# The first stretch of a two-layer f32 network on one core: three projection tiles in step, group 0's scan spread over two groups, lo halves on GpSimd

## The chip, the core and the metric

The kernel runs on one NeuronCore of a Trainium2 chip. The core has TensorE (PE: matrix products, operands from SBUF, results into PSUM), VectorE (DVE) and ScalarE (ACT) for elementwise work, GpSimd (POOL), and SyncE (SP), from whose queue nearly all transfers from device memory are issued. Each engine works through its own queue in order and waits on semaphores for the others. The metric is the device time of one execution in microseconds (us).

## The reference

Input x is 512 positions of 1024 features, f32. Two layers add to it, each on `rms_norm(h)`; a last norm follows. The first layer, the scan layer, is what the change touches:

```python
proj = u @ in_w                      # z, x, B, C and dt, side by side
xbc = silu(causal_depthwise_conv(xbc, conv_w, conv_b))
dt = softplus(dt_raw + dt_bias);  a = dt * -exp(a_log)
y = ssd_chunked(xs * dt[..., None], a, b_in, c_out)   # 4 chunks of 128, 32 heads, 8 groups
y = y + d_skip * xs
y = gated_group_rms_norm(y, z, norm_w, 8)
return y @ out_w
```

In a chunk, `ssd_chunked` multiplies the products of C and B by decays exp(cum(a)_t - cum(a)_s) and applies them to x; between chunks a state of 128 x 64 per head is carried on. The second layer is a latent attention with 16 heads, which the change leaves alone.

## The kernel before

**Numbers in two halves.** A weight or activation of 32 bits is cut into a high half (`hi`, a rounded copy by ACT, line 272 for weights) and a low half (`lo`, the difference by DVE, line 273). A product is three matmuls, hi x hi, hi x lo and lo x hi (`passes`). A tile of the projection, 128 output columns by 512 positions, is 8 blocks of 128 features and so 24 matmuls of 512 columns.

**Groups.** The scan layer has 8 groups. Each needs six tiles: B, C, x0, x1, z0, z1. `ssm_in(g)` issues these as a generator, six matmuls a step; `sched` runs it and starts other pieces of work when the matmuls issued so far (at 0.216 us each) reach a number in a table: `S0P` for the projection of group 0, `P0` for the work beside group 1's projection, `P1` for the later groups. These pieces are group g's scan (beside the projection of group g + 1): `cb` (transposes of B, products of C and B, decays L times cb), `x(0)` and `x(1)` (transposes, then `xdt` and `xw` on DVE), `states` (matmuls on `xw`, line 105, and the carried states S), and `y` (matmuls, lines 130 and 138, then the gate on DVE). `GN` places the group norm. So the order on every engine is written out by hand through these numbers; within it a scheduler may shift instructions on the other engines' queues.

**The first group.** The input's norm is not known at first. B, C, x0 to z1 of group 0, and the first four tiles of group 1, are computed from `vh`, `vl`, the halves of x times the norm's weight, and multiplied by 1/rms (`rr`, lines 322 to 324) when they leave PSUM. 1/rms comes from squares (ACT) summed on DVE, a product with ones on PE (`pssq`), a logarithm and an exponential on ACT, and three steps on DVE. `ssm_dt` computes dt in five steps; its first product `d`, times `rr`, is transposed on PE (line 504) before all the rest.

**Buffers.** Weights land in `raw` (2 buffers, 512 KB each, loaded from SP's queue at line 263). There are three `hi`, three `lo` buffers, and three PSUM banks for tiles (`mm`), three `aux`, two `yd`. `weight(i)` splits one tile ahead and loads one more. A `raw` buffer is free when both its halves are made, a `hi` buffer when PE has done the tile's 24 matmuls.

**The start.** x arrives as eight tiles; before, B and C of group 0 are computed together, x tile by x tile (`gemm2`, line 300), from weights that arrive in quarters of 128 KB per two x tiles. Then x0 follows on its own.

Of the kernel before, what the change touches and what calls it, by code (L numbers as in the profile page):

```python
# [10 lines left out]
F32 = mybir.dt.float32  # L11
F32R = mybir.dt.float32r
# [38 lines left out]
OA = 8  # L51
SQ = 2


# [97 lines left out]
class Net:  # L152
# [99 lines left out]
    def prefetch(self, want):  # L252
        while self.wload < min(want + 1, len(self.wq)):
            self.wraws.append(self.load_weight(*self.wq[self.wload]))
            self.wload += 1
        while self.wpos < min(want, len(self.wq)):
            self.wready[self.wq[self.wpos]] = list(self.split_weight(self.wraws.pop(0)))[-1]
            self.wpos += 1
# [6 lines left out]

    def split_weight(self, raw, cuts=()):
        nc = self.nc
# [3 lines left out]
        for a, b in zip((0, *cuts), (*cuts, n)):  # L271
            nc.scalar.copy(hi[:, a:b], raw[:, a:b])  # L272
            nc.vector.tensor_tensor(lo[:, a:b], raw[:, a:b], hi[:, a:b].bitcast(F32), op=ALU.subtract)  # L273
            yield
        yield hi, lo
# [19 lines left out]
    def gemm2(self, ps, ws, xh, xl, ks):  # L295
        seqs = [self.passes(w, xh, xl, ks) for w in ws]
        for k in range(ks):
            for p, seq in zip(ps, seqs):
                for i in range(3 * k, 3 * k + 3):
                    self.nc.tensor.matmul(p, seq[i][0], seq[i][1], start=i == 0, stop=i == 3 * ks - 1)  # L300
            yield 6 * 0.216

# [34 lines left out]
    def sumsq(self, tiles, n, pstag, pool=None, tags=("r0", "rt", "rr"), after=None):  # L337
        nc = self.nc
        acc = None
        for x in tiles:  # L340
# [19 lines left out]
    def ssm(self):  # L360
# [12 lines left out]
        self.wload = 2  # L373
        for k in range(KD):
            x = self.res.tile([P, T], F32, tag="res", name=self.nm("x"))
            nc.sync.dma_start(x[:], t["x"][k])
            self.xs.append(x)
            if k % 2 == 0:
                s = slice(k * P, (k + 2) * P)
                for i, raw in enumerate(raws):  # L380
                    nc.sync.dma_start(raw[:, s], t["w"][i, :, s])
        wdt = wk.tile([P, KD, NH], F32, name="wdt", bufs=1)
# [9 lines left out]

        vh, vl = [], []
        ws = [self.split_weight(raw, (256, 512, 768)) for raw in raws]
        for k in range(KD):
            a = self.o16.tile([P, T], F32R, tag="o", name=self.nm("vh"))
            b = self.o16.tile([P, T], F32R, tag="o", name=self.nm("vl"))
            last = nc.scalar.activation(a[:], self.xs[k][:], AF.Copy, scale=nw[:, k:k + 1])
            if k % 2 == 0:
# [6 lines left out]
        for i, w in enumerate(ws):  # L406
            self.wready[self.wq[i]] = next(w)
        self.wpos = 2
# [24 lines left out]
        for g in range(NG):  # L433
            ys, q = [], []
            pieces = [] if g == 0 else [(GN, late)]
            if g == 0:
                begin = lambda: q.append(SSD(self, 0, self.lexp(0), ys))
                pieces += [(SU[0] + SU[1] * k, scaled) for k in range(KD)]
                pieces += [(P0[0], step), (P0[1], step), (P0[1] + 0.1, begin)]
                at = P0[2:]  # L440
            else:
                q.append(SSD(self, g, self.lexp(g), ys))
                at = P1
            pieces += [(at[0], lambda: q[0].cb()), (at[1], lambda: q[0].x(0)), (at[2], lambda: q[0].x(1)),
                       (at[3], lambda: q[0].states()), (at[4], lambda: q[0].y())]
            if g + 1 < NG:
# [118 lines left out]
    def ssm_in(self, g, uh, ul, early):  # L565
# [3 lines left out]
        for i, (name, ct) in enumerate((("B", 16 + g), ("C", 24 + g), ("x0", 2 * g), ("x1", 2 * g + 1),  # L569
                                        ("z0", 0), ("z1", 0))):  # L570
            pair = (0, 1) if g == 0 and i < 2 else (4, 5) if g == NG - 1 and i >= 4 else None
            w = None if pair and i == pair[1] else self.weight("w", U_IN + 6 * g + i)
            xh, xl, r = early[:3] if i < early[3] else (uh, ul, None)
# [4 lines left out]
            if pair:  # L578
                if i == pair[0]:
                    two = [ps, self.mm()]  # L580
                    ws = [w, self.weight("w", U_IN + 6 * g + i + 1)]
                    yield from self.gemm2([p[:] for p in two], ws, xh, xl, KD)
# [489 lines left out]
```

## Time and profile before

| | |
|---|---|
| median of 3 runs | 840.74 us (840.42 to 841.0) |
| the profiled execution | 840.15 us, span 838.3 |
| PE busy, share of span | 822.8 us, 98% |
| DVE busy | 640.2 us, 76% |
| ACT busy | 453.5 us, 54% |
| POOL busy | 0.2 us, 4 instructions |

The page gives busy time per engine, waits by pair of instructions, and groups of like instructions by source line; the timeline gives single instructions with their start, length, and, in brackets, how long the engine was idle before and who released it. PE's instructions are pipelined, so the distance of their starts tells more than their length. Tile names are shown without their buffer numbers. DMA rows of SP show the issue; the time to landing is in the list of DMA issues.

### The profile page before, as it was taken

How to read it: one execution, taken by the hardware profiler on the slowest of the kernel's cores; microseconds unless marked ns; L12 is line 12 of the kernel's file. 1: busy time of each engine (PE TensorE's matmuls, PEld its weight loads, DVE VectorE, ACT ScalarE, POOL GpSimd, SP SyncE). 2: the span in 40 equal slices, each digit the busy share in tenths (PEclk: the TensorE clock that was granted, in tenths of full speed). 3: DMA queues.
4: the chain of work that ended last, by engine and by line, in shares of the span. 5: the costliest groups of instructions: out<-in, count | busy, mean ns of one | idle time of the engine just before them, and what ended most of it. 6: DMA issues, size and time to landing. Idle time of an engine off the chain costs nothing.

```text
span 838.3 us, 11586 instructions
## 1 busy us (share of the span) xinstructions
PE 822.8 (98%) x4260; PEld 694.8 (83%) x4260; DVE 640.2 (76%) x1226; ACT 453.5 (54%) x802; POOL 0.2 (0%) x4
## 2 busy tenths in 40 slices
PE   7999999999999999999999999999999999999996
PEld 5887888888888888888888888888888888888885
DVE  7899898979788979776564887786767869675544
ACT  7567755545565657333354664456547557554233
POOL 0000000000000000000000000000000000000000
PEclk9999999999999999999999999999999999999999
DMA  6354543434242424323225242222221224331212
GB/s 227 102 186 145 153 150 106 147 101 128 98 151 76 151 87 137 121 95 101 90 86 176 79 129 64 77 65 73 73 64 56 89 75 157 100 100 53 92 59 100
DMA packets 35112, 90.55 MB, mean 108 GB/s; under 512 B 4784, under 2 KB 6320, under 8 KB 35056
## 3 DMA queue, kind: packets, MB, share of 16 engines
q1 hardware_dynamic: 34336, 88.77, 32.9%
q10 hardware_dynamic: 720, 1.05, 0.3%
q8 instruction: 33, 0.54, 0.3%
q14 instruction: 23, 0.19, 0.1%
HBM read 83.12 MB, written 4.33 MB: 104 GB/s over the span
## 4 chain that ended last, share of the span: by engine, by line
PE 91%; DVE 5%; DMA 2%; ACT 1%; issue 1%; SPq 0%; DVEq 0%; ACTq 0%
PE mm L291 54%; PE ot L942 11%; PE s L794 5%; PE mm L300 4%; PE po L836 4%; PE mm L774 3%; PE pt L818 2%; PE yd L138 2%; PE yd L291 1%; PE aux L130 1%; PE aux L105 1%; DMA x<-in_x_dram 1%; PE aux L77 1%; PE aux L89 1%; DMA L<-ac_d 1%; DVE wlo L273 1%
## 5 line engine op out<-in xcount | busy, mean ns | idle before, releaser
L272 ACT CAST whi<-raw 128x1024 fp32r<-128x1024 f32 (+3 forms) x132 | 127.0, 965 | 214.7 <-PE mm L291 177.4
L273 DVE TENSOR_TENSOR wlo<-raw,whi 128x1024 fp32r<-128x1024 f32 (+3 forms) x132 | 146.8, 1115 | 56.1 <-ACT whi L272 55.8
L291 PE MATMUL mm<-ah,whi 128*128 128x512 f32 x384 | 153.9, 401 | 0.0
L291 PE MATMUL mm<-ah,wlo 128*128 128x512 f32 x384 | 150.1, 391 | 0.4 <-DVE wlo L273 0.4
L291 PE MATMUL mm<-al,whi 128*128 128x512 f32 x384 | 149.8, 390 | 0.0
L291 PE MATMUL mm<-vh,whi 128*128 128x512 f32 x224 | 89.6, 400 | 0.9 <-ACT whi L272 0.9
L291 PE MATMUL mm<-vh,wlo 128*128 128x512 f32 x224 | 87.8, 392 | 0.7 <-DVE wlo L273 0.7
L291 PE MATMUL mm<-vl,whi 128*128 128x512 f32 x224 | 87.5, 391 | 0.0
L291 PEld LDWEIGHTS mm<-ah,wlo 128*128 128x128 f32 x384 | 72.1, 188 | 16.0 <-DVE wlo L273 0.8
L291 PEld LDWEIGHTS mm<-ah,whi 128*128 128x128 f32 x384 | 72.2, 188 | 15.5 <-issue 1.4
L291 PEld LDWEIGHTS mm<-al,whi 128*128 128x128 f32 x384 | 72.2, 188 | 14.4 <-DVE al L312 0.3
L942 PE MATMUL ot<-whi,ah 128*128 128x512 f32 (+1 forms) x136 | 52.3, 384 | 0.0
L942 PE MATMUL ot<-whi,al 128*128 128x512 f32 (+1 forms) x136 | 51.4, 378 | 0.0
L942 PE MATMUL ot<-wlo,ah 128*128 128x512 f32 (+1 forms) x136 | 51.4, 378 | 0.0
L291 PEld LDWEIGHTS mm<-vh,wlo 128*128 128x128 f32 x224 | 42.0, 188 | 10.8 <-DVE wlo L273 1.5
L291 PEld LDWEIGHTS mm<-vh,whi 128*128 128x128 f32 x224 | 42.1, 188 | 9.2 <-ACT whi L272 1.1
L223 ACT ACTIVATE p<-p,st 128x128 f32<-128x128 f32 (+1 forms) x64 | 36.1, 564 | 25.1 <-DVE st L806 25.0
L291 PEld LDWEIGHTS mm<-vl,whi 128*128 128x128 f32 x224 | 42.2, 188 | 7.2
L822 ACT CAST ph<-pt 128x512 fp32r<-128x512 f32 (+1 forms) x64 | 26.5, 422 | 33.2 <-PE pt L818 32.8
L291 PE MATMUL mm<-ch,whi 128*128 128x512 f32 x104 | 42.6, 409 | 0.0
L291 PE MATMUL mm<-ch,wlo 128*128 128x512 f32 x104 | 40.8, 392 | 0.0
L291 PE MATMUL mm<-cl,whi 128*128 128x512 f32 x104 | 40.7, 392 | 0.0
(225 smaller groups left out, 1642.6 us busy)
## 6 DMA issues: line engine op xcount, KB each, us to landing
raw<-in_w_dram SPq DMA_DIRECT2D x100, 512.0 KB, 3.3
L<-ac_d SPq DMA_DIRECT2D x32, 256.0 KB, 3.8
E<-ea_d SPq DMA_DIRECT2D x32, 128.0 KB, 3.3
raw<-in_ua_dram SPq DMA_DIRECT2D x8, 512.0 KB, 3.3
raw<-in_ub_dram SPq DMA_DIRECT2D x8, 320.0 KB, 2.9
x<-in_x_dram SPq DMA_DIRECT2D x8, 256.0 KB, 4.3
res<-in_x_dram SPq DMA_DIRECT2D x8, 256.0 KB, 3.3
hd<-ht SPq DMA_DIRECT2D x8, 256.0 KB, 2.3
```

The lines of the kernel that those rows point to most:

```text
L138: nc.tensor.matmul(yd[64 * h:64 * h + 64, s], self.xdt[j][:, c, h, :], self.L[2 * j + h][:, s], start=True, stop=True)
L223: i = self.nc.scalar.activation(out, in_, func, **k)
L272: nc.scalar.copy(hi[:, a:b], raw[:, a:b])
L273: nc.vector.tensor_tensor(lo[:, a:b], raw[:, a:b], hi[:, a:b].bitcast(F32), op=ALU.subtract)
L291: self.nc.tensor.matmul(ps, a, b, start=i == 0, stop=i == len(seq) - 1)
L300: self.nc.tensor.matmul(p, seq[i][0], seq[i][1], start=i == 0, stop=i == 3 * ks - 1)
L774: nc.tensor.matmul(ps[:, c2 * 256:(c2 + 1) * 256], a, b, start=i == 0, stop=i == 5)
L794: nc.tensor.matmul(ps[:, :n], x[:, s], y[:, :n], start=k == 0, stop=k == 4)
L818: nc.tensor.transpose(pt[:, (b - kb) * P:(b - kb + 1) * P], probs[h][b][:, kb * P:(kb + 1) * P], self.ident)
L822: nc.scalar.copy(ph[:, :n], pt[:, :n])
L836: nc.tensor.matmul(po[:, kb * P:], x, y, start=kb == 0 and k == 0, stop=kb == NCH - 1 and k == 2)
L942: nc.tensor.matmul(ps[:, a:b], x, y, start=start and i == 0, stop=stop and i == 5)
```

## The change

Four things change together.

1. In the first stretch B, C and x0 of group 0 go in step (`gemm2` on three tiles). The third weight's quarters land in two activation buffers that are not in use yet. The squares of x are interleaved with the splitting instead of following it.
2. Eight matmuls on a tile of zeros (128 x 128) stand at the head of PE's queue.
3. Group 0's scan is spread: `cb`, `x(0)`, `x(1)` stay in group 1's projection, but later; `states` and `y` move to group 2's, where group 1's whole scan also follows later than before (`PL`, `PM`, `GM`). dt's steps move too (`S0P`, `P0`).
4. The lo halves of the other 45 weight tiles of the scan layer's projection are subtracted by POOL instead of DVE (`prefetch`, `split_weight`).

```diff
-S0P = (13.82, 14.2, 15.4, 15.6, 17.62)
+S0P = (15.5, 15.51, 15.52, 15.53, 24.2)
 SU = (0.64, 1.42)
-P0 = (6.0, 6.8, 11.91, 15.25, 17.25, 24.88, 34.5)
+P0 = (12.5, 14.0, 19.4, 22.5, 24.0)
+PL = (2.0, 7.0)
+PM = (12.0, 13.4, 14.8, 21.0, 27.0)
+GM = 29.5
...
+            engine = self.nc.gpsimd if self.wpos < 6 * NG else self.nc.vector
+            self.wready[self.wq[self.wpos]] = self.split_weight(self.wraws.pop(0), engine)
...
+        self.nc.scalar.copy(hi[:], raw[:])
+        engine.tensor_tensor(lo[:], raw[:], hi[:].bitcast(F32), op=ALU.subtract)
+        return hi, lo
...
-                self.link(i, [after])
+                self.link(i, [after[k]])
...
+        idle = wk.tile([P, P], F32, name="idle", bufs=1)
+        nc.vector.memset(idle[:], 0.0)
+        pw = aux()
+        for _ in range(WARM):
+            nc.tensor.matmul(pw[:, :P], idle[:], idle[:], start=True, stop=True)
...
+        third = [self.act.tile([P, T], F32, tag=g, name=self.nm("raw")) for g in ("ah", "al")]
+        raws.append([third[k // 2][:, (k % 2) * 2 * P:(k % 2 + 1) * 2 * P] for k in range(KD // 2)])
...
-            pss = self.sumsq([x[:] for x in self.xs], D, "aux", after=last)
+            pss = self.sumsq([x[:] for x in self.xs], D, "aux", after=[marks[min(k + 3, KD - 1)] for k in range(KD)])
...
+            elif g == 1:
+                pieces += [(PL[0], lambda: first[0].states()), (PL[1], lambda: first[0].y()), (PL[1] + 0.1, begin)]
+                at = PM
...
-            pair = (0, 1) if g == 0 and i < 2 else (4, 5) if g == NG - 1 and i >= 4 else None
+            pair = (0, 1, 2) if g == 0 and i < 3 else (4, 5) if g == NG - 1 and i >= 4 else None
```

The instructions as they stand on the engines, at three places. First, ACT's queue around the logarithm that starts 1/rms (`r<-pssq`). The casts of weight tiles around it make their `hi` halves: before, `whi_188`, `whi_242`, `whi_396` are those of x0, x1 and z0 of group 0. Before:

```order
L272 CAST whi_188<-raw_182 128x1024
L342 ACTIVATE sq_293<-x_113 128x512
L272 CAST whi_242<-raw_186 128x1024
L342 ACTIVATE sq_296<-x_115 128x512
L342 ACTIVATE sq_299<-x_119 128x512
L353 CAST sqh_302<-sqa_277 128x512
L272 CAST whi_396<-raw_240 128x1024
L223 ACTIVATE r_54_309<-pssq_306 128x512
L223 ACTIVATE r_54_309<-r_54_309 128x512
L272 CAST whi_434<-raw_394 128x1024
```

And now, where `whi_216`, `whi_381`, `whi_455` are x1, z0, z1:

```order
L355 ACTIVATE sq_338<-x_136 128x512
L275 CAST whi_216<-raw_212 128x1024
L366 CAST sqh_341<-sqa_316 128x512
L275 CAST whi_381<-raw_214 128x1024
L275 CAST whi_455<-raw_379 128x1024
L227 ACTIVATE r_56_348<-pssq_345 128x512
L227 ACTIVATE r_56_348<-r_56_348 128x512
L275 CAST whi_488<-raw_453 128x1024
```

In both, three weight casts precede the logarithm; they are now those of the tiles x1, z0 and z1, and the squares end ahead of them.

Second, SP's queue at the loads of these tiles, with the semaphores that each waits for (DVE, Pool: the engine that made the halves from the buffer's last content; DMAHW: earlier transfers). Before:

```order
L263 DMA raw_182<-in_w_dram 128x1024 [waits DMAHW6_49,DVE_49]
L263 DMA raw_186<-in_w_dram 128x1024 [waits DMAHW7_49,DVE_49]
L263 DMA raw_240<-in_w_dram 128x1024 [waits DMAHW6_49,DMAHW0_49,DVE_49]
L263 DMA raw_394<-in_w_dram 128x1024 [waits DMAHW7_49,DMAHW1_49,DVE_49]
L263 DMA raw_432<-in_w_dram 128x1024 [waits DMAHW2_49,DMAHW0_49,DVE_49]
```

Now:

```order
L268 DMA raw_212<-in_w_dram 128x1024 [waits DMAHW2_49,DVE_49]
L268 DMA raw_214<-in_w_dram 128x1024 [waits DMAHW3_49,DVE_49]
L268 DMA raw_379<-in_w_dram 128x1024 [waits DMAHW4_49,DMAHW2_49,Pool_49]
L268 DMA raw_453<-in_w_dram 128x1024 [waits DMAHW5_49,DMAHW3_49,Pool_49]
L268 DMA raw_486<-in_w_dram 128x1024 [waits DMAHW6_49,DMAHW4_49,Pool_49]
```

From the third load on they wait for POOL instead of DVE.

Third, SP's queue at the loads of group 1's decays (`L<-ac_d`, broadcast from device memory). Before, they stand behind loads of weight tiles that wait for DVE and ACT; `PE` is the last reader of the four L buffers:

```order
L263 DMA raw_838<-in_w_dram 128x1024 [waits DMAHW3_49,DVE_49,Activation_49]
L263 DMA raw_949<-in_w_dram 128x1024 [waits DMAHW0_49,DMAHW4_49,DVE_49,Activation_49]
L263 DMA raw_1018<-in_w_dram 128x1024 [waits DMAHW5_49,DMAHW3_49,DVE_49]
L627 DMA L_919<-ac_d 128x512 [waits DMAHW6_49,PE_49]
L627 DMA L_927<-ac_d 128x512 [waits DMAHW7_49,PE_49]
```

Now:

```order
L268 DMA raw_885<-in_w_dram 128x1024 [waits DMAHW7_49,Pool_49]
L268 DMA raw_934<-in_w_dram 128x1024 [waits DMAHW1_49,DMAHW0_49,Pool_49]
L268 DMA raw_1042<-in_w_dram 128x1024 [waits DMAHW7_49,Pool_49]
L268 DMA raw_1111<-in_w_dram 128x1024 [waits DMAHW2_49,DMAHW0_49,Pool_49]
L653 DMA L_995<-ac_d 128x512 [waits DMAHW3_49,DVE_49,PE_49]
L653 DMA L_1003<-ac_d 128x512 [waits DMAHW4_49,DVE_49,PE_49]
```

They stand behind the loads of group 2's x0, x1, z0 and z1 (`raw_885` to `raw_1111`), each of which waits for POOL.

More of the change, by code (lines that the diff above doesn't have):

```diff
@@ L52 @@
 SQ = 2
+WARM = 8
 class SSD:
@@ L264, in load_weight, with split_weight @@
         return raw
[L266 to L267 removed]
+    def split_weight(self, raw, engine):
         n = raw.shape[1]
@@ L270, in split_weight, with split_first @@
         lo = self.wlo.tile([P, n], F32R, tag="lo", name=self.nm("wlo"))
-        for a, b in zip((0, *cuts), (*cuts, n)):
-            nc.scalar.copy(hi[:, a:b], raw[:, a:b])
-            nc.vector.tensor_tensor(lo[:, a:b], raw[:, a:b], hi[:, a:b].bitcast(F32), op=ALU.subtract)
+        self.nc.scalar.copy(hi[:], raw[:])
+        engine.tensor_tensor(lo[:], raw[:], hi[:].bitcast(F32), op=ALU.subtract)
+        return hi, lo
+    def split_first(self, raw):
+        nc = self.nc
+        hi = self.whi.tile([P, D], F32R, tag="hi", name=self.nm("whi"))
+        lo = self.wlo.tile([P, D], F32R, tag="lo", name=self.nm("wlo"))
+        for k, part in enumerate(raw):
+            s = slice(2 * k * P, 2 * (k + 1) * P)
+            nc.scalar.copy(hi[:, s], part)
+            nc.vector.tensor_tensor(lo[:, s], part, hi[:, s].bitcast(F32), op=ALU.subtract)
             yield
@@ L339, in sumsq @@
         acc = None
-        for x in tiles:
+        for k, x in enumerate(tiles):
             sq = self.nrm.tile([P, T], F32, tag="sq", name=self.nm("sq"), bufs=SQ)
@@ L570, in ssm_in @@
                                         ("z0", 0), ("z1", 0))):
-            pair = (0, 1) if g == 0 and i < 2 else (4, 5) if g == NG - 1 and i >= 4 else None
-            w = None if pair and i == pair[1] else self.weight("w", U_IN + 6 * g + i)
+            pair = (0, 1, 2) if g == 0 and i < 3 else (4, 5) if g == NG - 1 and i >= 4 else None
+            w = None if pair and i != pair[0] else self.weight("w", U_IN + 6 * g + i)
             xh, xl, r = early[:3] if i < early[3] else (uh, ul, None)
@@ L579, in ssm_in @@
                 if i == pair[0]:
-                    two = [ps, self.mm()]
-                    ws = [w, self.weight("w", U_IN + 6 * g + i + 1)]
+                    two = [ps] + [self.mm() for _ in pair[1:]]
+                    ws = [w] + [self.weight("w", U_IN + 6 * g + k) for k in pair[1:]]
                     yield from self.gemm2([p[:] for p in two], ws, xh, xl, KD)
```

28 lines of the change are left out of this document (15 added, 13 removed).

## The prediction

> **What bounds the kernel now.** I read the head of the page first, then TensorE's (PE's) waits, then busy time by stretch.
>
> ```profile
> span 838.3 us, 11586 instructions
> PE 822.8 (98%) x4260; PEld 694.8 (83%) x4260; DVE 640.2 (76%) x1226; ACT 453.5 (54%) x802; POOL 0.2 (0%) x4
> ...
> PE mm L300 <- ACT whi L272: 4.8, 1, 4.8
> PE mm L291 <- DVE wlo L273: 1.0, 3, 0.5
> PE aux L105 <- DVE xw L94: 0.9, 1, 0.9
> PE mm L291 <- ACT whi L272: 0.9, 2, 0.7
> PE aux L504 <- DVE d L500: 0.2, 1, 0.2
> ...
> 126.00:294.00 168.00, 168.00 (x900) 141.01 (x899) 143.98 (x259) 94.19 (x143) 0.00 (x0) 1.00 0.37 120
> ```
>
> PE is busy 98% of the span and waits 7.8 us in all. Between 126 and 294 us (third to sixth group of the scan) it never stops, although VectorE (DVE, the third pair in the windows row) is busy 143.98 of 168 us. So taking work off DVE there is worth nothing by itself; only the holes before about 85 us can be won. The timeline of PE shows them:
>
> ```profile
> 4.77 0.80 PE L300 MATMUL mm<-vh,whi 128*128 128x512 f32 x1 [4.77 <-ACT whi L272]
> ...
> 7.99 0.63 PE L300 MATMUL mm<-vl,whi 128*128 128x512 f32 x1
> 8.42 0.63 PE L300 MATMUL mm<-vh,wlo 128*128 128x512 f32 x1
> ...
> 9.24 0.39 PE L300 MATMUL mm<-vl,whi 128*128 128x512 f32 x1
> 9.47 0.40 PE L300 MATMUL mm<-vh,wlo 128*128 128x512 f32 x1
> ...
> 17.64 0.39 PE L300 MATMUL mm<-vh,wlo 128*128 128x512 f32 x1
> 18.69 0.50 PE L291 MATMUL mm<-vh,whi 128*128 128x512 f32 x1 [0.66 <-ACT whi L272]
> 19.02 0.40 PE L291 MATMUL mm<-vl,whi 128*128 128x512 f32 x1
> 19.95 0.50 PE L291 MATMUL mm<-vh,wlo 128*128 128x512 f32 x1 [0.53 <-DVE wlo L273]
> ...
> 77.43 0.39 PE L291 MATMUL mm<-ah,wlo 128*128 128x512 f32 x1
> 78.69 1.56 PE L105 MATMUL aux<-xw,BT 128*128 128x256 f32 x6 [0.87 <-DVE xw L94]
> ...
> 80.32 0.40 PE L291 MATMUL mm<-al,whi 128*128 128x512 f32 x1
> 81.08 0.50 PE L291 MATMUL mm<-ah,wlo 128*128 128x512 f32 x1 [0.37 <-DVE wlo L273]
> ```
>
> Starts of 512-column matmuls lie 0.43 us apart at 8 us and 0.23 at 9.3 and after. The holes: the slow pace to 9 us; 0.8 + 0.7 us at 17.64 and 19.02 (distance less 0.23), where tile x0's weight is not split yet; 1.0 us at 77.43 and 0.5 us at 80.32.
>
> **The change part by part.**
>
> *Three tiles in step.* B, C and x0 go through the eight x tiles together, 9 matmuls per x tile instead of 6: 2.04 us at the 0.227 that the 24 starts from 35.48 to 40.92 (rows further below) lie apart. The 24 matmuls of x0 move ahead of the place where they waited, so 0.8 + 0.7 us go (they are within the 35.48 us below). The first start stays at 4.77: the same three transfers lead SP's queue. The second x tile stands behind one more issue:
>
> ```profile
> 1.17 0.90 SPq L381 DMA_DIRECT2D raw<-in_w_dram  x2
> ...
> 6.22 0.72 ACT L398 ACTIVATE vh<-x,nw 128x512 fp32r<-128x512 f32 x1 [0.63 <-DMA x<-in_x_dram]
> ...
> 6.97 1.64 DVE L402 SCALAR_TENSOR_TENSOR vl<-x,nw,vh 128x512 fp32r<-128x512 f32 x2 [0.93 <-ACT vh L398]
> ...
> 8.53 0.75 DVE L273 TENSOR_TENSOR wlo<-raw,whi 128x256 fp32r<-128x256 f32 x2
> ```
>
> A row with x2 is two instructions. The second x tile lands 0.90 / 2 = 0.45 us later: vh from 6.7 to 7.4, vl to 8.1. From there 8 matmuls, five x tiles and B's three of the last: 8.1 + 8 x 0.227 + 5 x 2.04 + 0.7 = 20.8 us, when B's weight buffers come free. DVE's splitting before that, 8 x 0.75 + 12 x 0.38 = 10.6 us by the rows above and below, with half of the squares' sums, hides behind these matmuls, and ScalarE's (ACT) likewise; a tile split late would hold PE by what it is late.
>
> *Eight matmuls on zeros.* They only bring the fast pace forward. No row shows them so early; if the pace stayed slow to 9.2 us as now, about 1 us is lost on the 20.8; if they ran into 4.77, about as much. I take 0 and keep 0 to +1.
>
> *The square root's turn.* ACT's order puts the cast of tile z1's weight (whi_455) ahead of the logarithm that starts 1/rms. That cast needs the load raw_379, which now waits for GpSimd (POOL) to finish the first lo half, wlo_217. All else for the first stretch hangs on this:
>
> ```profile
> 17.61 1.03 ACT L272 CAST whi<-raw 128x1024 fp32r<-128x1024 f32 x1
> ...
> 25.31 0.60 ACT L223 ACTIVATE r<-pssq 128x512 f32<-128x512 f32 x1 [0.67 <-PE pssq L357]
> ...
> 28.78 0.69 DVE L500 TENSOR_TENSOR d<-aux,rr 128x512 f32<-128x512 f32 x1
> ...
> 29.53 0.66 PE L504 MATMUL aux<-ident,d 128*128 128x128 f32 x4 [0.16 <-DVE d L500]
> 29.94 0.48 PE L291 MATMUL yd<-vh,whi 128*128 128x512 f32 x1
> ...
> 35.48 0.39 PE L291 MATMUL yd<-vh,whi 128*128 128x512 f32 x1
> ...
> 40.92 0.39 PE L291 MATMUL mm<-vh,whi 128*128 128x512 f32 x1
> ...
> raw<-in_w_dram SPq DMA_DIRECT2D x100, 512.0 KB, 3.3
> ```
>
> Cast of x1's weight when B's buffer is free, 20.9 to 22.0; lo half g; load 3.3 and its issue 0.1; cast 1.05; logarithm to the first matmul behind the transposes as now, 29.94 - 25.31 = 4.63: 31.1 + g. That matmul is z0's first; now z0's first is the one at 35.48. PE alone would be there at 20.8 + (6 + 18 + 24) x 0.227 + 0.45 = 32.1. So this stretch wins 35.48 - (31.1 + g) = 4.4 - g us, at most 3.4, and PE stands before the transposes for g - 1.0 us.
>
> *What g is.* POOL ran four memsets here; the trace has no such subtraction. The bounds, from DVE:
>
> ```profile
> L273 DVE TENSOR_TENSOR wlo<-raw,whi 128x1024 fp32r<-128x1024 f32 x26 | 31.7, 1220 | 18.1 <-ACT whi L272 18.1
> ...
> 39.94 0.94 DVE L520 RECIPROCAL dy<-dy 128x128 f32<-128x128 f32 x1
> ```
>
> Below, the same subtraction, 1.22 us; above, DVE's dearest elementwise row, 0.94 us for 128 columns, 8 x 0.94 = 7.5 us. I take 2.5, nearer the row of the same operation: this stretch wins 1.9 us (3.1 to a loss of 3.1).
>
> [...]
>
> *The other 45 lo halves.* A cast for tile i + 1 waits for PE to leave tile i - 2, two tiles or about 10.9 us (48 x 0.227) ahead of need. 1.05 + g is hidden in that up to g = 9; the two raw buffers turn in (3.3 + 1.05 + 0.4 + g) / 2, under 5.4 us a tile up to g = 6. At 2.5 nothing reaches PE. DVE loses 31.7 of 143.98 us and the 18.1 us in which its queue stood behind a lo half waiting for ACT.
>
> *Group 0's scan in group 1.* Its states matmuls stand 42 matmuls behind the last x transposes (36 now), 1.4 us later against a wait of 1.0, and B's lo half at 81.08 no longer stands in DVE's queue: I take both holes as gone, 1.5 us (0 to 1.5). In return group 1's scan starts late: its L loads stand in SP's queue behind raw_1111, which waits for the lo half of x1 of group 2. From the L loads on, now:
>
> ```profile
> 93.99 1.57 ACT L632 ACTIVATE L<-L,ac 128x128 f32<-128x128 f32 x5 [1.91 <-DMA L<-ac_d]
> ...
> 102.62 0.55 DVE L94 TENSOR_TENSOR xw<-xdt,dec 128x384 f32<-128x384 f32 x1
> ...
> L<-ac_d SPq DMA_DIRECT2D x32, 256.0 KB, 3.8
> ...
> L610 DVE SCALAR_TENSOR_TENSOR x<-mm,cols,x 128x509 f32<-128x509 f32 x9 | 6.6, 738 | 0.0
> ```
>
> From the landed L to xw 103.2 - 94.0 = 9.2 us. PE's z0 starts at 33.6 (g = 2.5); nine tiles on, B of group 2 ends near 33.6 + 216 x 0.227 + 5 for the small matmuls = 87.6. Then cast 1.05, lo half 2.5, issues 0.5, L loads 3.8: 95.5, and about 1.5 later, as the raw tile before it waits for a lo half too. With 9.2 and some five conv rows of 0.74 in the same queue xw comes near 110; PE, 78 matmuls (17.7) and about 5 us of small ones after 87.6, asks near 110. I take a new wait of 1.0 us, with bounds 0 and 2.6, the excess of two lo halves over 1.22.
>
> *Sum.* The profiled execution took 840.15 us (its span 838.3 and 1.85 around it). 840.15 - 1.9 - 1.5 + 1.0 = 837.75, or 2.4 less. The median of the runs is 840.74; the same step from there gives **838.3 us**.
>
> **The rivals.**
>
> *The lo half costs 3 to 3.7 us: no change.* The stretch wins 4.4 - g, and the new wait grows by two for each of g. At g = 3.3: 1.1 + 1.5 - (1.0 + 1.6) = 0: 840.7. For it: nothing in the trace fixes g inside its bounds. Against: it is the same simple operation as the 1.22 us row.
>
> *It costs over 3.7: slower.* At g = 4.1: 0.3 + 1.5 - (1.0 + 3.2) = -2.4, or 843.1. It decides from g = 3.9.
>
> *POOL blocks DVE: slower.* While POOL reads, DVE instructions wait. From 126 to 294 DVE has 143.98 - 31.7 = 112.3 us left; 26 lo halves are 65 us; blocked for a share s of them DVE needs 112.3 + 65 s, and 168 is full at s = 0.86. At s = 0.95 it is 174, 6 us over, 9 us for the whole scan (about 250 us): 838.3 + 9 = 847. For it: L by cb, the dearest group left, reads two tensors from SBUF. Against: the conv rows above read PSUM, and a share over 0.86 needs nearly every instruction blocked.
>
> ```profile
> L81 DVE TENSOR_TENSOR L<-L,cb 128x512 f32<-128x512 f32 x16 | 10.0, 686 | 4.0 <-ACT L L223 4.0
> ```
>
> [...]
>
> **How the numbers follow.** Forecast 0.52, lo half of 3 to 3.7 us 0.24, over 3.7 us 0.12, DVE blocked 0.12. Below 0.2% (1.7 us) a measurement of this kernel cannot tell a change from none. So faster 0.52, same 0.24, slower 0.24. Low end: g = 1.22 (-1.3), no new wait (-1.0), and 0.5 for the reading of rows: 835.5. High end: past 843.1 and 1 us for a clock that comes late: 844.5, leaving out most of the last rival. The forecast's own range is 836 to 839.5.
>
> **What would show it.** The lo halves on POOL at 2 to 3 us; PE waiting at the transposes of d for 1 to 2 us, released by DVE's d, with whi_455's cast right ahead of the logarithm; matmuls at 0.23 us before 8 us; no wait at group 0's states, one of about 1 us at group 1's; no PE wait from 126 us on. It is wrong if PE never waits at those transposes (the chain through raw_379 is then not the path), if lo halves exceed 3.7 us, or if DVE's rows grow longer beside POOL's.

## The result, and the profile after

The changed kernel took **861.52 us** (median of 4 runs, 860.52 to 866.31) against 840.67 of the kernel before in the same session. The ratio is 1.026, with a 95% interval of 1.022 to 1.030: slower. The forecast was 838.3 us and faster.

The head of the profile's page of the changed kernel and PE's waits (engine and line that waited, what released it, us in total, times, the longest):

```profile
span 858.7 us, 11663 instructions
PE 831.1 (97%) x4276; PEld 701.8 (82%) x4276; DVE 643.0 (75%) x1185; ACT 453.8 (53%) x805; POOL 111.8 (13%) x49
...
PE aux L579 <- ACT acT L570: 8.3, 1, 8.3
PE aux L109 <- DVE xw L98: 4.8, 1, 4.8
PE aux L75 <- ACT B L236: 4.1, 1, 4.1
PE aux L530 <- issue: 1.3, 1, 1.3
```

The first row to notice is DVE's: 45 subtractions of 1.22 us were taken from it, and it is busy 643.0 us, 2.8 us more than before. Then there are three new waits of PE, 17.2 us together. None of them is for a lo half: they are for group 0's decays (acT, at 60 us), group 1's `xw` (at 122 us) and the silu of group 2's B (at 145 us).

Beside or right behind each of these waits lies a stretch in which the clock granted to PE is half (0.50). Busy time by stretch around the first one, and then the other two stretches at half clock (us from the start, then length, PE busy, PEld, DVE, ACT, POOL, granted clock, DMA share and GB/s):

```profile
62.87:73.11 10.24, 3.95 (x14) 3.47 (x15) 10.21 (x14) 3.75 (x7) 2.56 (x1) 0.50 0.49 146
73.11:84.00 10.89, 10.89 (x57) 9.14 (x56) 8.53 (x14) 7.85 (x20) 2.40 (x1) 1.00 0.73 237
127.72:131.14 3.42, 3.42 (x9) 2.69 (x10) 3.15 (x7) 0.62 (x1) 0.00 (x0) 0.50 0.46 153
148.21:155.03 6.82, 5.32 (x19) 4.62 (x20) 4.82 (x9) 6.79 (x11) 0.00 (x0) 0.50 0.00 1
```

In these three stretches PE is busy 3.95 + 3.42 + 5.32 = 12.7 us. The starts of 512-column matmuls lie 0.43 us apart in them (152.55 to 154.26 us) and 0.23 at full clock (131.29 to 131.98), so about half of the 12.7 us is work: 6.3 us are lost beside the waits. The end of the first stretch, in PE's timeline:

```profile
33.44 0.63 PE L530 MATMUL aux<-ident,d 128*128 128x128 f32 x4 [1.29 <-issue]
33.83 0.48 PE L304 MATMUL yd<-vh,whi 128*128 128x512 f32 x1
```

z0's first matmul starts at 33.83, where it was at 35.48. The profile names no releaser for the wait of 1.29 us before the transposes; DVE's `d` ends at 33.34. That closes the account against the kernel before: -1.65 for the first stretch, -1.5 for the two old holes, +17.2 for the waits, +6.3 for the half clock, +20.4 us in sum; the spans differ by 858.7 - 838.3 = 20.4.

### The profile page after: what moved, and what is told of

It is laid out like the page before. It is cut to its first block, busy times and chain, and to the rows that moved or that the text cites. A ratio compares the mean times of both kernels' runs of the same rounds, so it can differ in the third digit from the quotient of the medians.

```text
span 858.7 us, 11663 instructions
## 1 busy us (share of the span) xinstructions
PE 831.1 (97%) x4276; PEld 701.8 (82%) x4276; DVE 643.0 (75%) x1185; ACT 453.8 (53%) x805; POOL 111.8 (13%) x49
## 4 chain that ended last, share of the span: by engine, by line
PE 86%; DVE 8%; ACT 2%; DMA 2%; issue 1%; POOL 0%; SPq 0%; ACTq 0%; DVEq 0%; POOLq 0%
PE mm L304 50%; PE ot L968 10%; PE mm L313 5%; PE s L820 5%; PE po L862 3%; PE mm L800 3%; PE pt L844 2%; PE yd L142 2%; DMA L<-ac_d 2%; PE aux L109 1%; PE aux L134 1%; DVE x L636 1%; DVE L L85 1%; DVE B L636 1%; PE aux L81 1%
## 5 line engine op out<-in xcount | busy, mean ns | idle before, releaser
L275 ACT CAST whi<-raw 128x1024 fp32r<-128x1024 f32 (+2 forms) x123 | 122.9, 1001 | 196.3 <-PE mm L304 118.0
L276 POOL TENSOR_TENSOR wlo<-raw,whi 128x1024 fp32r<-128x1024 f32 x45 | 111.6, 2483 | 222.9 <-ACT whi L275 222.9
L276 DVE TENSOR_TENSOR wlo<-raw,whi 128x1024 fp32r<-128x1024 f32 (+2 forms) x78 | 87.6, 1125 | 33.6 <-ACT whi L275 33.4
L304 PE MATMUL mm<-vh,whi 128*128 128x512 f32 x216 | 86.6, 401 | 0.0
L304 PE MATMUL mm<-vh,wlo 128*128 128x512 f32 x216 | 84.8, 393 | 0.1
L304 PE MATMUL mm<-vl,whi 128*128 128x512 f32 x216 | 84.8, 393 | 0.0
```

The costliest lines, as they stand in the source:

```text
L275: self.nc.scalar.copy(hi[:], raw[:])
L276: engine.tensor_tensor(lo[:], raw[:], hi[:].bitcast(F32), op=ALU.subtract)
L304: self.nc.tensor.matmul(ps, a, b, start=i == 0, stop=i == len(seq) - 1)
```

## Why VectorE is held: the rows of the changed kernel

The mean length of DVE's groups between 126 and 294 us, by shape, in the changed kernel:

```profile
L660 DVE TENSOR_SCALAR L<-L,ac 128x128 f32<-128x128 f32 x48 | 16.9, 414 | 3.1 <-DMA L<-ac_d 3.1
L85 DVE TENSOR_TENSOR L<-L,cb 128x512 f32<-128x512 f32 x16 | 14.4, 960 | 6.6 <-ACT L L227 6.6
L98 DVE TENSOR_TENSOR xw<-xdt,dec 128x384 f32<-128x384 f32 x9 | 10.5, 1197 | 0.1
L636 DVE SCALAR_TENSOR_TENSOR x<-mm,cols,x 128x509 f32<-128x509 f32 x8 | 5.9, 736 | 0.0
L148 DVE TENSOR_TENSOR E<-aux,E 128x384 f32<-128x384 f32 x8 | 4.4, 551 | 3.7 <-PE aux L134 3.6
```

And the same groups in the kernel before (L by cb, 686 ns, and the conv row, 738, stand in the prediction):

```profile
L634 DVE TENSOR_SCALAR L<-L,ac 128x128 f32<-128x128 f32 x60 | 12.6, 277 | 0.0
L144 DVE TENSOR_TENSOR E<-aux,E 128x384 f32<-128x384 f32 x8 | 4.4, 550 | 0.0
L94 DVE TENSOR_TENSOR xw<-xdt,dec 128x384 f32<-128x384 f32 x8 | 4.1, 549 | 0.0
```

The two groups with both inputs in SBUF have grown (L by cb 686 to 960, xw 549 to 1197), the two with an input in PSUM (`mm`, `aux`) have not (738 and 736, 550 and 551). The convolution, L636, shows both sides by itself: with its input `mm` in PSUM no row of it lasts over 0.75 us, with `raw` in SBUF (groups 0 and 1) it lasts up to 2.89. L660, with one tile as input, grew too (277 to 414): three of its 48 rows last 2.49 to 2.50 us, each ending with a subtraction of POOL, and the others 0.27 to 0.29. So here a row with one input in SBUF was held as well. What it looks like singly, at the place of the first wait (timelines of POOL, DVE, ACT and PE, each piece in order of time):

```profile
51.43 4.80 POOL L276 TENSOR_TENSOR wlo<-raw,whi 128x1024 fp32r<-128x1024 f32 x2 [8.53 <-ACT whi L275]
62.93 2.56 POOL L276 TENSOR_TENSOR wlo<-raw,whi 128x1024 fp32r<-128x1024 f32 x1 [6.70 <-ACT whi L275]
...
51.60 2.39 DVE L552 SCALAR_TENSOR_TENSOR dq<-dq,dy 128x128 f32<-128x128 f32 x1
54.02 2.36 DVE L553 SCALAR_TENSOR_TENSOR dt<-dz,dq 128x128 f32<-128x128 f32 x1
...
62.55 3.49 DVE L636 SCALAR_TENSOR_TENSOR B<-raw,cols,B 128x511 f32<-128x511 f32 x2
...
68.00 0.62 ACT L324 CAST ah<-u 128x512 fp32r<-128x512 f32 x1 [4.63 <-DVE u L447]
68.53 0.58 ACT L570 COPY acT<-aux 128x512 f32<-128x512 f32 x1
...
60.45 0.39 PE L304 MATMUL mm<-vh,wlo 128*128 128x512 f32 x1
69.16 1.11 PE L579 MATMUL aux<-ident,acT 128*128 128x128 f32 x4 [8.32 <-ACT acT L570]
```

The last two steps of dt, on 128 columns, last until POOL's two subtractions end, 2.4 us each. (Beside idle POOL, in the run e11 below, such a row takes 0.29.) The next subtraction, at 62.93, holds a row of B's convolution in the same way: two rows take 3.49 us for 1.5. Everything behind them on DVE, the scaled halves `u` included, is late; ACT's casts of `u` stand ahead of its copy of acT, so that copy waits 4.63 us for a `u`; and PE, whose transposes of acT stand 6 matmuls behind the product of `a`, stands for 8.3 us.

How full DVE was there before shows in one row, 32 to 92 us, of the kernel before; then the same of the changed one:

```profile
32.00:92.00 60.00, 58.76 (x309) 48.72 (x308) 56.81 (x100) 39.81 (x65) 0.00 (x0) 1.00 0.47 148
```

```profile
32.00:92.00 60.00, 50.39 (x233) 41.80 (x233) 56.95 (x83) 35.38 (x59) 17.42 (x7) 0.91 0.41 132
126.00:294.00 168.00, 162.40 (x849) 135.71 (x850) 139.04 (x226) 89.71 (x137) 56.93 (x24) 0.97 0.34 110
```

In groups 0 and 1 DVE was 95% busy, ten lo halves (12.2 us) among it; the changed kernel has none of them on DVE there, gets less other work done, and DVE is as busy as before. Six held rows account for that, the two of dt and those at 40.56, 63.33, 74.93 and 87.28 us: together they are 12.2 us longer than such rows beside idle POOL, for seven subtractions of POOL.

## The experiments

**1. Each part undone or done alone.** The first four, and the first stretch alone.

*e1: every lo half on VectorE, all else as changed.*

```diff
-            engine = self.nc.gpsimd if self.wpos < 6 * NG else self.nc.vector
+            engine = self.nc.vector
```

> The change with all lo halves left on DVE. Theory A (POOL's reads hold DVE instructions with two SBUF inputs, and DVE's lateness makes PE's three long waits of 8.3, 4.8 and 4.1 us): the three waits go, matmuls stay at full clock, the stretch to z0's first matmul wins about 3 us as a lo half is 1.2 us long; 836 to 839 us. Rival B (the moved pieces of group 0's and 1's scan ask too early whatever makes the lo halves): at least two of the three waits stay above 3 us, and the time is 850 to 862 us.

Measured 846.48 us, ratio to before 1.006 (1.005 to 1.008). So 15.0 of the 20.9 us are GpSimd's, and the time lies between the two expectations. Of these 15.0, 1.5 us are the later start of z0 (33.83 for 32.37 here), which the forecast had counted; the rest it had not. PE's waits:

```profile
PE mm L304 <- DVE wlo L276: 5.2, 3, 3.3
PE aux L75 <- ACT B L236: 3.5, 1, 3.5
```

The waits for acT and xw are gone, so they were GpSimd's. The wait for B's silu stays, and three for lo halves are new, so the rest of the change costs something of its own.

*e2: the kernel before, with the lo halves of tiles 2 to 47 on GpSimd alone.*

```diff
-            nc.vector.tensor_tensor(lo[:, a:b], raw[:, a:b], hi[:, a:b].bitcast(F32), op=ALU.subtract)
+            (engine or nc.vector).tensor_tensor(lo[:, a:b], raw[:, a:b], hi[:, a:b].bitcast(F32), op=ALU.subtract)
```

> The kernel before with POOL making the lo halves of tiles 2 to 47, nothing else changed. Theory A: DVE rows with two SBUF inputs grow to about 2.4 us where a lo half runs, and PE waits several us in the first two groups; 846 to 862 us. Rival B (only the moved pieces are at fault): DVE has room, no new PE wait over 2 us; 839 to 842 us.

Measured 850.88 us, ratio 1.012 (1.011 to 1.014). GpSimd alone costs 10.4 us in the old order as well, as theory A had it. Some 2.7 us of it arise before z0 (its first matmul is at 38.22 for 35.48): with two tiles in step PE waits there for the lo half itself. The rest lies at the same place as in the changed kernel:

```profile
PE aux L554 <- ACT acT L545: 7.8, 1, 7.8
...
PE mm L292 <- POOL wlo L274: 1.7, 1, 1.7
```

*e3: GpSimd from the fourth group's tiles on.*

```diff
-            engine = self.nc.gpsimd if self.wpos < 6 * NG else self.nc.vector
+            engine = self.nc.gpsimd if 18 <= self.wpos < 6 * NG else self.nc.vector
```

> The change with POOL making lo halves only from tile 18 on (group 3's projection and later), DVE the earlier ones. Theory A, with the harm done where DVE has no room: the waits near 60 and 122 us go, what is left is small; 836 to 842 us. If blocking hurts the later groups as well, 845 us or more. Rival B: as the change, 855 us or more.

One run of 851.51 us. The waits for acT and xw are gone as in e1; the one for B's silu is longer than in e1 (5.7 for 3.5), with a row of 2.62 us on DVE at 121 us, where GpSimd's tiles begin:

```profile
PE aux L75 <- ACT B L236: 5.7, 1, 5.7
```

The time is in the range set for a hold that hurts the later groups too (845 or more), but e1, without GpSimd, is there already. Nor can the distance of this one run from e1 be put to GpSimd alone: 1.8 us of the 3.5 between the two profiles arise before GpSimd can have acted, at a wait of 2.5 us for a lo half of VectorE (1.8 in e1) and 3.4 us at half clock from 117.68 us on.

Behind the third wait the hold costs next to nothing. From one and the same matmul (at 160.12 us in the changed kernel, 147.99 in e1) to the last one, it takes 691.2 us in the changed kernel, 690.8 in e1, 691.2 in e3 and 691.8 in e4: 0.4 to 1.0 us for the rest of the 45 subtractions.

*e4: the lo half in four GpSimd instructions of 256 columns.*

```diff
-        engine.tensor_tensor(lo[:], raw[:], hi[:].bitcast(F32), op=ALU.subtract)
+        step = 256 if engine is self.nc.gpsimd else n
+        for c in range(0, n, step):
+            engine.tensor_tensor(lo[:, c:c + step], raw[:, c:c + step], hi[:, c:c + step].bitcast(F32), op=ALU.subtract)
```

> The change with each lo half on POOL cut into four instructions of 256 columns. [...]

One run of 857.9 us. The pieces take 841 ns each (GpSimd's group of the trace):

```profile
L278 POOL TENSOR_TENSOR wlo<-raw,whi 128x256 fp32r<-128x256 f32 x180 | 145.5, 841 | 186.1 <-ACT whi L275 181.6 <-DMA raw<-in_w_dram 3.3 <-PE aux L109 1.1
```

No DVE row before 400 us is longer than 1.25 us, where the changed kernel has rows of 2.89: with GpSimd's instruction at 841 ns for 2483 the longest row is shorter too. The wait for xw falls to 1.2 us, but the one for acT is still 7.0, and the one for B's silu grows to 4.9. Between 32 and 92 us there are 30 pieces for 7 subtractions, and GpSimd is busy 27.4 us for 17.4. The lo half is also done later, which moves z0's first matmul to 35.12.

*e8: the first stretch alone: three tiles in step and the zeros, lo halves on VectorE, the old scan.*

```diff
-P0 = (12.5, 14.0, 19.4, 22.5, 24.0)
+P0 = (6.0, 6.8, 11.91, 15.25, 17.25, 24.88, 34.5)
...
-            pieces = [] if g == 0 else [(GM if g == 1 else GN, late)]
+            pieces = [] if g == 0 else [(GN, late)]
...
-            elif g == 1:
-                pieces += [(PL[0], lambda: first[0].states()), (PL[1], lambda: first[0].y()), (PL[1] + 0.1, begin)]
-                at = PM
```

> The first stretch of the change alone: three tiles in step and the matmuls of zeros, every lo half on VectorE, group 0's whole scan in group 1's projection at the numbers of the kernel before, the gated norms all at 16.84. Theory A: the first stretch wins what the forecast said with a lo half at VectorE's price (4.4 less 1.2, so 3.2 us), the two old waits of 1.5 us stay: 837.5, 836 to 839. Theory B: the start is taken back by a later wait, since VectorE and ScalarE have the same work to do in less time before group 1's scan: 840 to 846, with a new wait of 2 us or more between 40 and 120 us.

Measured 841.97 us, ratio 1.002 (1.001 to 1.003): theory B. z0's first matmul stands at 32.65, 2.8 us earlier than before, and the gain is gone by 55 us:

```profile
PE aux L563 <- DVE a L557: 3.7, 1, 3.7
...
PE aux L109 <- DVE xw L98: 0.8, 1, 0.8
```

So the change, put together in this order, splits into three: the first stretch +1.5 us (before to e8), the spread of the scan +4.5 (e8 to e1), GpSimd +15.0 (e1 to the changed kernel). In another order the parts differ: in the kernel before, GpSimd costs 10.4 (e2).

**2. Is it the hold, or a late lo half?**

*e9: every lo half on VectorE, and spare work on GpSimd beside it.*

```diff
+        if self.wpos < 6 * NG:
+            self.nc.gpsimd.tensor_tensor(self.spare[:, :n], hi[:].bitcast(F32), hi[:].bitcast(F32), op=ALU.subtract)
```

> The changed kernel with every lo half on VectorE, and beside each of the 45 a subtraction of the same size on GpSimd (hi less hi, 1024 columns) whose result nobody reads: it is extra work that is not part of the computation, and its output is unused. So no tile waits for GpSimd. Theory A: the loss comes from GpSimd's holding of VectorE, whoever needs the result: against the run with the lo halves on VectorE alone (846.5) it is slower by 10 us or more, 856 to 875, and VectorE rows with two SBUF inputs last 2 to 2.9 us here and there. Theory B: the loss comes from the lo halves being late on GpSimd (2.4 us against 1.2): the spare work costs nothing, 845 to 848.

Measured 874.23 us, ratio 1.041 (1.039 to 1.043); 27.7 us over e1, which differs in nothing but work whose result nobody reads (one cast of ACT waits 1.7 us for a buffer that this work still reads). So the hold by itself is enough for such a loss. In the changed kernel, too, no wait of PE is for a lo half of GpSimd; its lateness counts in the 1.5 us at z0, and perhaps in 1.2 us of the wait for xw (e4). The size of 27.7 is not that of the changed kernel's loss, as VectorE keeps its own 45 subtractions here. DVE's own lo half, two inputs in SBUF, now takes 1601 ns on average for 1218 in e1, and the conv rows are as they were (126 to 294 us):

```profile
L276 DVE TENSOR_TENSOR wlo<-raw,whi 128x1024 fp32r<-128x1024 f32 x24 | 38.4, 1601 | 1.4 <-ACT whi L275 1.4
L639 DVE SCALAR_TENSOR_TENSOR x<-mm,cols,x 128x510 f32<-128x510 f32 (+2 forms) x23 | 17.0, 738 | 0.1
```

**3. The third wait.** PE's transposes of group 2's B wait for a silu that stands on ACT behind the loads of L, the logarithm and exponential of group 0's norm, and a table load. In the changed kernel's timeline of ACT:

```profile
143.93 1.29 ACT L658 ACTIVATE L<-L,ac 128x128 f32<-128x128 f32 x4 [7.65 <-DMA L<-ac_d]
...
145.63 0.58 ACT L227 ACTIVATE r<-pssq 128x512 f32<-128x512 f32 x1
...
146.63 0.62 ACT L227 ACTIVATE r<-r 128x512 f32<-128x512 f32 x1
...
147.74 1.28 ACT L236 ACT_TABLE_LOAD   x1
149.03 0.63 ACT L236 ACTIVATE B<-B 128x512 f32<-128x512 f32 x1
```

I took the norm's place for the cause, and moved it forward, in the changed kernel (e5) and in e1 (e6):

```diff
-GM = 29.5
+GM = 16.84
```

> The changed kernel with the gated norm of group 0 at 16.84 us of group 2's projection, as every other group has it, where the change put it at 29.5; the lo halves stay on GpSimd. Theory A: the third wait of the changed kernel (4.1 us before PE's transposes of B in group 3's feed, L75) is made by this place, since ScalarE's silu of B stands behind the norm's Ln and Exp; it goes, and with it the 6.8 us at half clock that follow it (3.4 us of work lost): 861.5 - 4.1 - 3.4 = 854, 851 to 856; the waits of 8.3 and 4.8 us at 60 and 122 us stay. Theory B: VectorE, held by GpSimd, makes the third wait too, and it only moves: 858 to 863.

> The changed kernel with every lo half on VectorE and the gated norm of group 0 at 16.84 us of group 2's projection. Theory A (three separate causes: GpSimd's hold on VectorE, the norm's place, the clock behind each wait): against the run with the lo halves on VectorE alone (846.5) the wait of 3.5 us goes and the 6.8 us at half clock with it (3.4 us): 839.5, 837.5 to 842; that is the kernel before or a little under it. Theory B: the spread of group 0's scan costs something of its own in any schedule: 844 to 848, with the waits of 3.3 us for lo halves at 80 us and 2 to 4 us at 114 and 134 us still there.

Measured 866.69 us (ratio 1.031, 1.030 to 1.033) and 851.18 us (1.013, 1.012 to 1.015): each about 5 us slower than without the edit. My theory fell. The wait for B's silu goes, and a longer one comes for the squares of group 0's y. PE's waits in e5 and in e6:

```profile
PE pssq L369 <- ACT sqh L366: 12.0, 1, 12.0
PE aux L579 <- ACT acT L570: 8.2, 1, 8.2
```

```profile
PE pssq L369 <- ACT sqh L366: 8.9, 1, 8.9
PE mm L304 <- DVE wlo L276: 3.3, 2, 3.2
```

With group 0's y moved to 7.0 us of group 2's projection, its norm cannot be had at 16.84; at 29.5 it holds up the next group's silu. I tried no place between. So the price belongs to the spread in this schedule, 4.5 us from e8 to e1. The rows above allow an estimate of the shares: between the end of the L rows (145.22) and the table load (147.74) lie 2.5 us of the norm and its neighbours, so without them some 1.6 of the 4.1 us would remain, for the L loads that ACT stood idle for (7.65 us). No run tests this.

**4. The zeros.** *e7: e6 without its eight matmuls; e13: the kernel before with them alone.*

```diff
-WARM = 8
+WARM = 0
```

> The run before this one without its eight matmuls of zeros at the start. Theory A: they only bring the full clock forward (4.85 us against 9.19 us in the kernel before), in a stretch in which PE waits for the input tile by tile: the first 31 us lose 0 to 1 us, so 0 to 1 us slower than the run with them. Theory B: three tiles in step leave no slack for matmuls at half clock between 4.8 and 9.2 us, and all 4.3 us at half clock are lost work: 2 to 3 us slower.

> The kernel before with the eight matmuls of zeros alone: two tiles in step, lo halves on VectorE, the old scan. Theory A: the full clock comes at 4.8 to 6.5 us for 9.2 and PE reaches z0 0.5 to 1.2 us earlier, but VectorE is full from 32 to 80 us and takes it back: 840.4 within 0.8. Theory B: what the first stretch wins comes out at the end, as the difference of 2.1 us between the two runs with and without the zeros says: 838.0 to 839.4.

e7 took 853.27 us, 2.1 more than e6, with z0's first matmul 1.3 us later (33.65 for 32.32): they are worth something with three tiles in step. The time is that of theory B, where I had leaned to 0 to 1. e13 took 839.95 us, ratio 0.9995 (0.9985 to 1.0005), no difference: full clock came at 6.0 us for 9.2, and z0 still started at 35.49 for 35.48, as with two tiles in step PE is not what the first stretch waits for.

**5. Why the first stretch alone wins nothing.**

*e10 and e11: e8 with dt's steps, and what follows them, moved back by what PE had gained.*

```diff
-P0 = (6.0, 6.8, 11.91, 15.25, 17.25, 24.88, 34.5)
+P0 = (10.5, 11.5, 15.0, 17.0, 19.0, 29.0, 36.0)      # e10
+P0 = (10.5, 11.5, 15.0, 17.0, 19.0, 26.0, 34.5)      # e11
```

> The first stretch of the change alone, lo halves on VectorE, with the steps of group 0's scan in group 1's projection moved back by what PE has gained: 10.5, 11.5, 15, 17, 19, 29, 36 for 6, 6.8, 11.91, 15.25, 17.25, 24.88, 34.5. Theory A: the new wait of 3.7 us (PE's product of a with the triangle, L563, for VectorE's rows of dt) and the 6.8 us at half clock behind it were the whole reason why the first stretch alone won nothing: 842.0 - 3.7 - 3.4 = 834.9, 834 to 837.5, no wait over 1.5 us from 40 to 130 us. Theory B: VectorE's work of group 0's scan has no slack, and the wait comes back at the states (xw, L109) or at y or at the next group's B: 839 to 843.

> As the run before this one, but with the states at 26 and y at 34.5, near the old numbers. Theory A: the wait was dt's alone, and the states' rows (xw) are ready in time: 834 to 837.5. Theory B: the states now come before xw is ready: a wait of 2 to 5 us at L109, with half clock behind it, 839 to 843.

845.20 us (1.006, 1.005 to 1.008) and 842.45 us (1.002, 1.001 to 1.003): in theory B's range in e11, above both in e10. Moving the request away moved the wait, to a lo half that neither theory had named. In e11:

```profile
PE mm L304 <- DVE wlo L276: 3.2, 2, 3.0
PE aux L576 <- ACT acT L567: 1.4, 1, 1.4
PE aux L93 <- DVE ac L578: 1.2, 1, 1.2
```

*e12: e11 without the lo halves of tiles 3 to 14.*

```diff
...
+        if 3 <= self.wpos < 15:
+            return hi, hi
         engine.tensor_tensor(lo[:], raw[:], hi[:].bitcast(F32), op=ALU.subtract)
```

> As the run before (first stretch alone, lo halves on VectorE, dt's steps later), but the lo halves of the projection's tiles 3 to 14 are not computed: the matmuls read the hi half in their place, so these tiles' products are not the reference's. This takes 12 x 1.22 = 14.6 us of VectorE's work out of 32 to 92 us and leaves PE's and ScalarE's as they are. Theory A: VectorE is full from 32 to 92 us (11.1 to 12.0 us busy of each 12) and alone takes back what the first stretch won: the waits there (3.0 for a lo half, 1.4 for acT, 1.2 for ac) and the half clock behind them (1.7 of work) go: 842.5 - 7.3 = 835, 833.5 to 837. Theory B: the waits are the order of ScalarE's and PE's work: acT's and ac's stay and move, 839 to 843.

Measured 836.31 us, ratio 0.995 (0.993 to 0.997): 6.1 us under e11, where 7.3 were expected of theory A. Between 20 and 480 us only the wait for acT (1.4) is left, no stretch there is at half clock, and DVE is busy 51.73 of 60 us:

```profile
32.00:92.00 60.00, 58.57 (x314) 49.26 (x313) 51.73 (x97) 44.21 (x76) 0.00 (x0) 1.00 0.52 165
```

PE's and ScalarE's orders were left as they were, and at 92 us PE is still 3.2 us ahead of the kernel before. So it is VectorE's work between 32 and 92 us that takes the first stretch back. The run leaves one thing together: 4.5 of its 6.1 us are the wait for a lo half and the half clock around it, and such a wait cannot come where no lo half is made. That the load counts and not only this row, e15 below shows: there all lo halves are made, 1.1 us of other work leaves VectorE, and the wait falls from 3.0 us to 0.2 at most.

*e14, e15, e16: the load moved, not dropped.* e14 computes all six tiles of group 1 from the unscaled halves, so that the scaled ones come later; e15 gives ScalarE the fourth head's decays; e16 does both. All start from e11.

```diff
-MID = 4
-SU = (0.64, 1.42)
+MID = 6
+SU = (0.64, 3.2)
...
-LA = (3, 1)
+LA = (4, 1)
```

> The first stretch alone with dt's steps moved back, lo halves on VectorE, and all six tiles of group 1 computed from the unscaled halves of x (four before), so that the eight scaled halves (u, al: 8 x 0.74 + 8 x 0.68 = 11.4 us of VectorE) are due a whole group later and are spread, one each 3.2 us for 1.42. It adds two multiplications by 1/rms on VectorE (1.4 us). Theory A: VectorE's load between 44 and 80 us is what takes the first stretch back; some 5 us of it move behind 80 us, where PE has waited for nothing: the waits there (3.0 for a lo half, 1.4, 1.2) shrink by 3 to 5 us and the half clock goes: 836 to 839. Theory B: VectorE is as full behind 80 us as before it, the waits move there: 841 to 845.

> As the run with dt's steps moved back (842.5), with the fourth head's four decay rows of groups 0 and 1 on ScalarE, which has 19 of 60 us free there: 4 x 0.27 = 1.1 us a group off VectorE, same results. Theory A: each us off VectorE before 92 us is a us off the waits: 840.5 to 842. Theory B: ScalarE's queue is the one that is late: 842.5 to 844.

> Both of the edits before in one kernel. Theory A: 835.5 to 838.5, faster than the kernel before. Theory B: 841 to 845.

844.48 us (1.006, 1.004 to 1.007), 839.97 (0.9999, 0.999 to 1.001) and 841.88 (1.002, 1.001 to 1.003). Moving work a little later within groups 0 and 1 (e14) is worse: it adds two DVE rows, and one lo half is waited for 4.2 us (theory B, as in e16). Taking 1.1 us a group off DVE (e15) wins 2.5 us against e11, somewhat more than theory A had.

*e17 and e18: e15 with PE's requests placed nearer to DVE's results.*

```diff
-P0 = (10.5, 11.5, 15.0, 17.0, 19.0, 26.0, 34.5)
+P0 = (10.5, 12.9, 15.0, 18.5, 20.0, 24.9, 34.5)      # e17
+P0 = (10.5, 12.9, 14.5, 18.5, 19.5, 23.5, 34.5)      # e18
```

> As the run with the decays on ScalarE (840.0), with dt's second step at 12.9 for 11.5, x at 18.5 and 20 for 17 and 19 and the states at 24.9 for 26, so that PE asks for acT, ac and xw nearer to when they were ready and the carried states start earlier. Theory A: the four waits left (1.0 acT, 1.3 ac, 1.8 S; 4.1 us) and the one stretch of 3.4 us at half clock (1.7 of work) go in part: 835.5 to 838.5, faster than the kernel before. Theory B: VectorE is full, and each wait that goes is paid for at the next lo half or state: 839 to 842.

> As the run before this one, with cb at 14.5, x(1) at 19.5 and the states at 23.5. Theory A: 835.5 to 838.5, or a wait of about 1 us for xw at the states in its place. Theory B: 839 to 842.

840.38 us (1.0001, 0.999 to 1.001; theory B), and **838.63 us** for e18, ratio 0.9976 (0.9967 to 0.9985), between its two theories and with the wait for xw that A named. e18 beats both kernels, by 2 us and by 23. Its waits:

```profile
PE aux L134 <- DVE S L117: 1.4, 1, 1.4
PE aux L93 <- DVE ac L578: 1.2, 1, 1.2
PE aux L109 <- DVE xw L98: 1.0, 1, 1.0
```

It waits 3.6 us in three pieces and has no half clock behind any; e17 waits 2.4 us for S in one piece, and 3.4 us at half clock follow.

**The account over the runs.** With the terms of the first section, each against the kernel before, in us (profiled runs; waits of 0.3 us and less left out; "half clock" is half of PE's busy time in the stretches at 0.5):

| run | z0's first matmul | waits after it | half clock | old holes | sum | span, measured |
|---|---|---|---|---|---|---|
| changed | -1.65 | +17.2 | +6.3 | -1.5 | +20.4 | +20.4 |
| e1 | -3.1 | +8.7 | +4.4 | -1.5 | +8.5 | +8.0 |
| e8 | -2.8 | +4.5 | +2.6 | -1.5 | +2.8 | +2.4 |
| e11 | -3.1 | +5.8 | +1.5 | -1.5 | +2.7 | +2.1 |
| e18 | -3.1 | +3.6 | 0 | -1.5 | -1.0 | -1.2 |

## Why the prediction was wrong, by its own steps

- **Three tiles in step, the square root's turn, g.** Right. The first start is at 4.67 (4.77 forecast), a lo half takes 2.48 us on GpSimd (2.5), the cast of x1's weight starts at 21.05 (20.9) and that of z1's at 27.81 (27.9), PE stands before the transposes of d for 1.3 us (1.5), and z0 starts at 33.83 (33.6). The stretch wins 1.65 us (1.9).
- **The zeros at 0.** Right. The sum of 20.8 us took the fast pace from the start and put about 1 us on its not coming. With the zeros full clock came at 4.84 us, where it came at 9.19 before (starts of matmuls are 0.23 us apart from 5.83 us on, before from 9.24); without them, in e7, z0 starts 1.3 us later.
- **"At 2.5 nothing reaches PE."** This step failed. It asks when the lo half is there, and it is: no wait of PE names one on GpSimd. It does not ask what GpSimd does to VectorE while it works: rows of VectorE that read SBUF lasted up to 2.89 us, PE's waits for acT and xw, 13.1 us together, came in with it, and GpSimd's part cost 15.0 us (e1). The credit beside it, "DVE loses 31.7 of 143.98 us", did not come either: from 126 to 294 us DVE is busy 139.04, 24 x 1.22 = 29.3 us of subtractions fewer, but about 24 us of holds more.
- **The rival "POOL blocks DVE".** It was named, at 0.12, with the condition s, and it is what happened: rows of 0.29 us lasted 2.4 beside POOL's subtractions. In the trace before, POOL was busy 0.2 us, so nothing there showed it, and the 0.12 was the author's estimate. Its price was worked out in the wrong stretch. In 126 to 294 us s came out at about 24 / 56.93 = 0.43, under the 0.86 from which it decides, and indeed only 0.4 us are lost from 160 us on. But the condition was put on a stretch where DVE had 24 us free of 168. From 32 to 92 us it had 3.2 of 60, and there every step of dt, u and the scan is on the path from one PE piece to the next, so the length of one row matters, not the sum. The forecast read DVE's share from 126 us on and never between the first stretch and there. For the rival it named only L by cb, with two tensors from SBUF, where L660, with one, was held too (2.49 to 2.50 us for 0.27 to 0.29). The last of the prediction's signs of being wrong, longer DVE rows beside POOL's, is the one that came.
- **"I take both holes as gone", and the new wait of 1.0 at group 1's states.** The holes went. The wait at `xw` measured 4.8 us for 1.0 (0 to 2.6): two L by cb rows ahead of it last 2.40 and 2.22 us for 0.69, which makes 3.2 of it. In e4, where these rows are not held (0.73 and 0.67), it is 1.2, near the forecast; in e1 there is none. Not seen at all was the third wait, for B's silu behind the L loads and group 0's norm: 3.5 to 4.1 us, in e1 too.
- **The first stretch's win as a win.** "Only the holes before about 85 us can be won" counted an earlier z0 in full. e8, e11 and e12 show that PE was about to be bound by VectorE there: 2.8 to 3.1 us earlier at z0 came back as waits of 4.5 to 5.8.
- **The clock.** No term stood for it; the high end alone allowed 1 us. Behind the new waits 6.3 us were lost at half clock, more than any gain in the sum.

## What to carry to other kernels

Read the share of every engine in the stretch just behind a gain before counting it: VectorE, at 95% there (56.81 of 60 us), handed the gain back. Order alone then shifted the wait (e10, e11); order and 1.1 us a group taken off that engine kept 2 us of it (e18). Work moved to GpSimd was not taken off VectorE here, where both read SBUF: each subtraction took 1.22 us off and put about 1.0 us back between 126 and 294 us and 1.7 between 32 and 92, in single pieces of some 2 us, behind which PE waited 8.3 us where a chain of small VectorE rows is on the path. A longer wait of PE was dearer than its length, by the half clock beside it (10.24 us of it around the 8.3 us of the changed kernel); three short ones (e18, 3.6 us) cost less than the 3.7 us of e17 with one of 2.4 among them.

## What was not expected of the hardware

- A DVE row of 128 columns that takes 0.29 us beside idle GpSimd (e11) lasted 2.36 to 2.39 us beside a GpSimd subtraction of 1024 columns; beside pieces of 841 ns no row is longer than 1.25 us (e4). The pieces are dear: 4 x 841 = 3.4 us for 2.48.
- A subtraction whose result nobody reads cost 27.7 us in 45 instructions (e9), where VectorE kept its own 45; the useful one cost 15.0.
- The granted clock fell to 0.50 beside waits of PE. In the changed kernel it did so beside the waits of 8.3, 4.8 and 4.1 us (for 10.24, 3.42 and 6.82 us), in e1 beside 3.3 and 3.5 us (for 3.41 and 6.82), in e8 beside 3.7 us (for 6.83), in e11 beside 3.0 us (for 3.42), in e17 beside 2.4 us (for 3.4). It did not after 1.8 us in e1 (at 116.64 us), after 1.4 us in e12, or after 1.4, 1.2 and 1.0 us in e18. It did after pairs of 1.0 and 1.7 us in e2 (for 3.40) and of 1.3 and 0.5 in e15. In e11 it fell 0.4 us before the wait ended (80.94, the wait to 81.35), in e17 0.9 us after (86.89, the wait to 85.96). No run shows what sets its start and its length.
